# A list-scheduled decoder trunk: issue order by due times, other PSUM banks for one output projection, a token-tile-wise entry

## The chip, the cores and the metric

The kernel runs on one core of a Trainium2 chip. The metric is the device time of one execution in microseconds (us). Three executions of the kernel before took 1010.73, 1011.19 and 1012.37 us; their median, 1011.19 us, is the time that the change is compared with.

## The reference

The kernel computes a trunk of two layers on 256 tokens of 1024 channels, in float32. Each layer is an FFN, a token mixer and a second FFN; every one of these six parts reads a normalised copy of the residual stream h and adds a normalised result to it:

```python
def rms_norm(x, g):
    y = xf * lax.rsqrt(jnp.mean(xf * xf, axis=-1, keepdims=True) + NORM_EPS)
    return y * g
...
def swiglu(x, w_in, w_out):
    a, b = jnp.split(x @ w_in, 2, axis=-1)      # 1024 -> 2 * 2816
    return (jax.nn.silu(a) * b) @ w_out         # 2816 -> 1024
...
for l in range(DEPTH):                          # 2
    f = swiglu(rms_norm(h, g[0]), ffn1_w_in[l], ffn1_w_out[l])
    h = h + FFN_RES * rms_norm(f, g[1])
    hn = rms_norm(h, g[2])
    m = even_mixer(hn, ...) if l % 2 == 0 else odd_mixer(hn, ...)
    h = h + rms_norm(m, g[3])
    f = swiglu(rms_norm(h, g[4]), ffn2_w_in[l], ffn2_w_out[l])
    h = h + FFN_RES * rms_norm(f, g[5])
```

The even mixer is stick-breaking attention (8 heads) beside a causal depthwise convolution of width 31. The odd mixer is gated linear attention (4 heads, chunks of 64), whose output is normalised by head, multiplied by silu(r) and projected by w_out.

## The kernel before, in words

**Tiles.** The 256 tokens are two token tiles, A (t = 0) and B (t = 1), of 128 rows. Channels lie in eight blocks of 128. A float32 product is made of three fp32r matmuls (`mm3`, L334 to L336): high part by high part, low by high, high by low. So each weight tile of 128 x 1024 that arrives by DMA (raw, L318) is cast on ScalarE (ACT) to its high part (hi, L310), and VectorE (DVE) subtracts that from the tile to get the low part (lo, L311). Names in the trace follow: raw_fi, hi_fi and lo_fi are FFN input weights, fo its output weights, he and ho the even mixer's, gq, gv and gout the odd mixer's. Activations are split in the same way into uTh and uTl.

**Phases.** There are six: ffn0, even mixer, ffn1, ffn2, odd mixer, ffn3. In an FFN the first four of 22 column blocks are computed token-major: the matmuls fill a bank pt, the gate makes ut = silu(a) * b from it (ACT L582 or L587, DVE L584 or L588), TensorE (PE) transposes ut into a bank ptr (L595), and ACT and DVE split that into uTh and uTl. The other 18 blocks are computed channel-major into two banks pw_j0 and pw_j1 (L536 with the high weights, 512 columns; L538 with the low ones, 256 columns), gated through uab and uw, and split. The output projection o_f (L334 to L336) fills four banks, one for each token tile and half of the channels.

**Between the phases.** The post-norm of a token tile squares the four banks' halves on ACT (psq, L344), multiplies each half by the gain on DVE (py, L361), adds the two sums and eps (pst, L349), raises the sum to the power -1/2 on GpSimd (POOL, L340, a 128x1 tensor_tensor), and updates h (L367). The pre-norm then has the same chain (xsq, xst, the power, xn L467) and PE transposes xn into xT (xtr_p, L479).

**The entry.** ffn0 doesn't wait for statistics: class Entry multiplies the first four blocks by g * x^T, unnormalised (`split`: xgh L395 on ACT, xgl L397 on DVE, in blocks of 256 columns; matmuls pt<-hi_fi,xgh and so on), and the gate applies the row's rstd later. x itself (h) is loaded on the same DMA queue (`load_x`, L300), squared, and its rstd is laid out along rows by a matmul with the identity (rstd_rows, L425 and L427). `scaled` then multiplies x^T by gain and rstd (L432), casts (L442) and subtracts (L443); the channel-major blocks pw_40 and later read this xT.

**The odd mixer's end.** For each chunk and head the output bank go is squared (og L1064), its statistic gst gets eps (L1067) and the power (L340), sm = go * gst * rg (L1069), and sm is transposed (gt L1076) and split for the output projection o_go. Beside that DVE copies masked scores out of PSUM (COPY_PREDICATED, L1041).

**Memory rings.** PSUM has eight banks: four in the ring "out", two in the ring "in" (b0, b1; the projections' banks), two in the ring "tr" (b2, b3; transposes); channel-major blocks (ring "pw") take b0 to b3 in turn. Raw weights have four buffers, hi and lo parts nine.

**What sets the order.** The program isn't issued as it is written. Every step is recorded as an Op with an engine, a modelled cost in ns, the tiles it reads and writes, and a number i in program order. `Plan.schedule` then runs a list scheduler: the engine that can start earliest takes, among its ready steps (within a patience of some ns), the one with the lowest prio:

```python
o = min((o for o in ops if max(free[e], o.ready) <= t0 + o.patience), key=lambda o: o.prio)
```

prio is the number i, apart from a few steps that `urgent` sets ahead. The resulting order is fixed in the instruction streams: each engine and each queue works strictly in that order, and an instruction that waits holds all behind it on its engine. The costs and latencies of the model only choose the order.

## Time and profile before

| | |
|---|---|
| runs | 1010.73, 1011.19, 1012.37 us |
| the profiled execution | 1011.41 us |
| its span (first to last instruction on the core) | 1009.7 us |
| granted TensorE clock over the span, mean | 0.998 |
| PE busy | 992.0 us (98%) |
| DVE busy | 679.7 us (67%) |
| ACT busy | 568.0 us (56%) |
| POOL busy | 57.0 us (6%) |
| DMA | 180.46 MB, mean 179 GB/s |

The profile comes from one execution, which took 1011.41 us by the device's clock; 1.7 us of that lie outside the span. Busy times are sums of instruction durations; matmuls are pipelined, so the drawn end of one lies behind the start of the next. The chain that ended last follows the work back from the last instruction, at each step to what released it.

### The profile page before, as it was taken

Reading aid. Unit: us, or ns where it says so; the run is one execution under the profiler, and the core shown is the slowest. Engines: PE = TensorE matmul, PEld = TensorE weight load, DVE = VectorE, ACT = ScalarE, POOL = GpSimd, SP = SyncE. Lnnn points to the kernel's source line nnn. Section 1 sums busy time; section 2 is a strip of 40 time slices with the busy share of each in tenths; the row PEclk is TensorE's granted clock in tenths of the full one; section 3 lists DMA queues with packets and bytes.
Section 4 is the critical chain, followed back from the end, with each engine's and each line's share of the span. In section 5 each row is a group of like instructions: output and inputs, shape, how many; then the busy total and the mean of one; then the engine's idle time right before and its main releaser. Section 6 shows DMA issues by size and latency. Waiting matters only on the chain.

```text
span 1009.7 us, 13983 instructions
## 1 busy us (share of the span) xinstructions
PE 992.0 (98%) x5216; PEld 843.0 (83%) x5216; DVE 679.7 (67%) x1103; ACT 568.0 (56%) x979; POOL 57.0 (6%) x109
## 2 busy tenths in 40 slices
PE   7999999999999999999999999999999999999997
PEld 5888888888777888888888888888899887888885
DVE  5875668669868766667666566774588686656662
ACT  7764556575556655557455555664474375555551
POOL 2630000100001000000000000000001110000000
PEclk9999999999999999999999999999999999999999
DMA  9775557552035756566446465672551156555531
GB/s 326 236 249 191 191 203 258 184 184 68 22 126 167 255 170 221 166 211 228 169 161 216 167 218 161 228 267 69 191 205 64 42 188 230 187 188 191 198 112 42
DMA packets 50342, 180.46 MB, mean 179 GB/s; under 512 B 5713, under 2 KB 5969, under 8 KB 50274
## 3 DMA queue, kind: packets, MB, share of 16 engines
q1 hardware_dynamic: 50274, 179.57, 53.4%
q8 instruction: 41, 0.67, 0.3%
q14 instruction: 27, 0.22, 0.1%
HBM read 178.50 MB, written 1.05 MB: 178 GB/s over the span
## 4 chain that ended last, share of the span: by engine, by line
PE 90%; DVE 4%; DMA 2%; ACT 1%; issue 1%; POOL 1%; SPq 0%; DVEq 0%; POOLq 0%; ACTq 0%
PE pw L536 25%; PE pw L538 13%; PE o_f L334 8%; PE o_f L335 8%; PE o_f L336 8%; DMA raw_fi<-ffn_in 2%; PE pt L334 2%; PE pt L335 2%; PE pt L336 2%; PE gv L334 1%; PE gv L336 1%; PE gv L335 1%; PE cv L836 1%; PE xtr_p L479 1%; PE hq L334 1%
## 5 line engine op out<-in xcount | busy, mean ns | idle before, releaser
L536 PE MATMUL pw<-xT_p,hi_fi 128*128 128x512 f32 x1152 | 287.9, 392 | 2.3 <-DVE ut L588 1.3
L536 PEld LDWEIGHTS pw<-xT_p,hi_fi 128*128 128x128 f32 x1152 | 210.5, 188 | 43.8 <-DVE uTl L311 1.8
L311 DVE TENSOR_TENSOR lo_fi<-raw_fi,hi_fi 128x1024 fp32r<-128x1024 f32 (+1 forms) x177 | 212.8, 1217 | 47.8 <-ACT hi_fi L310 34.3
L310 ACT CAST hi_fi<-raw_fi 128x1024 fp32r<-128x1024 f32 (+1 forms) x177 | 181.4, 1046 | 40.1 <-DMA raw_fi<-ffn_in 19.4
L538 PEld LDWEIGHTS pw<-xT_p,lo_fi 128*128 128x128 f32 x1152 | 157.1, 190 | 11.3
L538 PE MATMUL pw<-xT_p,lo_fi 128*128 128x256 f32 x1152 | 160.6, 282 | 0.0
L662 DVE TENSOR_TENSOR uab<-pw,uab 128x256 f32<-128x256 f32 x144 | 60.8, 422 | 111.9 <-ACT uab L661 111.9
L661 ACT COPY uab<-pw 128x256 f32<-128x256 f32 x144 | 53.5, 372 | 130.7 <-PE pw L538 130.7
L334 PE MATMUL o_f<-hi_fo,uTh 128*128 128x512 f32 x224 | 88.2, 394 | 0.0
L335 PE MATMUL o_f<-lo_fo,uTh 128*128 128x512 f32 x224 | 87.8, 392 | 0.0
L336 PE MATMUL o_f<-hi_fo,uTl 128*128 128x512 f32 x224 | 87.2, 389 | 0.0
L311 DVE TENSOR_TENSOR lo_fo<-raw_fo,hi_fo 128x1024 fp32r<-128x1024 f32 x56 | 68.4, 1222 | 13.7 <-ACT uw L663 8.9
L310 ACT CAST hi_fo<-raw_fo 128x1024 fp32r<-128x1024 f32 x56 | 58.9, 1052 | 18.6 <-PE pw L536 11.9
L340 POOL TENSOR_TENSOR pst_p<-pst_p,mhalf 128x1 f32<-128x1 f32 x12 | 8.2, 685 | 783.5 <-DVE pst_p L349 768.8
L560 ACT CAST uTh<-uw 128x256 fp32r<-128x256 f32 x72 | 29.3, 407 | 38.8 <-DVE uw L664 38.6
L334 PE MATMUL o_f<-h_fo,uTh 128*128 128x512 f32 x128 | 50.8, 397 | 0.0
L336 PE MATMUL o_f<-h_fo,uTl 128*128 128x512 f32 x128 | 50.5, 395 | 0.0
L335 PE MATMUL o_f<-l_fo,uTh 128*128 128x512 f32 x128 | 50.5, 395 | 0.0
L336 PEld LDWEIGHTS o_f<-hi_fo,uTl 128*128 128x128 f32 x224 | 42.1, 188 | 9.2
L334 PEld LDWEIGHTS o_f<-hi_fo,uTh 128*128 128x128 f32 x224 | 42.3, 189 | 7.3
L335 PEld LDWEIGHTS o_f<-lo_fo,uTh 128*128 128x128 f32 x224 | 42.3, 189 | 6.7
L311 DVE TENSOR_TENSOR l_fo<-raw_fo,h_fo 128x1024 fp32r<-128x1024 f32 x32 | 39.1, 1223 | 10.0 <-ACT h_fo L310 9.7
(249 smaller groups left out, 1654.5 us busy)
## 6 DMA issues: line engine op xcount, KB each, us to landing
raw_fi<-ffn_in SPq DMA_DIRECT2D x176, 512.0 KB, 4.5
raw_fo<-ffn_out SPq DMA_DIRECT2D x88, 512.0 KB, 4.4
raw_gv<-gla_in SPq DMA_DIRECT2D x16, 512.0 KB, 4.6
...
```

Of the source, the lines that this page charges most:

```text
L310: act(n, lambda: nc.scalar.copy(hi(), src()), r, [w[0]], psum=psum)
L311: dve(n, lambda: nc.vector.tensor_sub(lo(), src(), hi().bitcast(F32)), list(r) + [w[0]], [w[1]])
L334: nc.tensor.matmul(ps, lhsT=lhs[0], rhs=rhs[0], start=start, stop=False)
L335: nc.tensor.matmul(ps, lhsT=lhs[0], rhs=rhs[1], start=False, stop=False)
L336: nc.tensor.matmul(ps, lhsT=lhs[1], rhs=rhs[0], start=False, stop=stop)
L479: nc.tensor.transpose(ps[:, k * P:(k + 1) * P], y[:, c * P:(c + 1) * P], ident[:, :])
L536: nc.tensor.matmul(pss[i][:, :], lhsT=wk, rhs=xT[:, k, :, :], start=k == 0, stop=False)
L538: nc.tensor.matmul(pss[i][:, S:], lhsT=wk, rhs=xT[:, k, 0, :], start=False, stop=k == KT - 1)
L560: act(n, lambda: nc.scalar.copy(h_[:, s], src()), r, [(h_, 0), (h_, 1)], psum=psum)
L661: act(S, lambda v=v, ps=ps: nc.scalar.copy(v(), ps[:, S:]), [ps], [(g, i)], psum=True)
L662: dve(S, lambda v=v, ps=ps: nc.vector.tensor_add(v(), ps[:, :S], v()), [ps, (g, i)], [(g, i)])
L836: nc.tensor.matmul(pv[:, :S], lhsT=d[:, o:o + P], rhs=pads(c)[:, i:i + S], start=i == 0, stop=i == CONV_PE - 1)
```

## The change

It has three parts.

1. **Order by due times.** After a first run in program order, `set_due` takes the PE order it gave, lays the PE steps end to end by their costs, and goes backward through all steps: a step is due when the earliest of its users is due, less the latency to that user and its own cost. prio of all steps but PE's becomes this due time, ties go by i, and the scheduler runs again; this is done twice (`PASSES`). PE keeps program order as its priority. Modelled constants change too: the latency from engine to engine from 80 to 150 ns, the one behind a DMA from 900 to 600, the DMA rate from 360 to 285 bytes per ns, the cost of the power from 470 to 690.
2. **Banks.** The output projection of the odd mixer takes tile A's two banks from the ring "in" in place of "out".
3. **Entry.** `split` works in halves of 512: ACT scales x^T in place by the gain (2 x 256), then one cast (512), and DVE subtracts once (512). `scaled` works by token tile: tile A's rstd_rows matmul, four-block products, casts and subtracts don't wait for tile B's. The product no longer has the gain in it, since x^T has it already. load_x(0) and load_x(1) stand around the weights of the second pair of blocks in program order.

```diff
+PASSES = 2
...
-    LATENCY = 80
-    DMA_START, DMA_DONE = 1700, 900
+    LATENCY = 150
+    DMA_START, DMA_DONE = 1700, 600
...
-        return self.add("dma", nbytes / 360.0, fn, r, w)
+        return self.add("dma", nbytes / 285.0, fn, r, w)
...
+        order = self.run()
+        for _ in range(PASSES):
+            self.set_due(order)
+            order = self.run()
+        return order
+
+    def latency(self, o, u):
+        lat = self.LATENCY if u.eng != o.eng or o.eng in ("act", "dve") else 0.0
+        return lat + (self.DMA_DONE if o.eng == "dma" else 0) + (self.DMA_START if u.eng == "dma" else 0)
+
+    def set_due(self, order):
+
+
+        t, begin = 0.0, {}
+        for o in order:
+            if not isinstance(o, str) and o.eng == "pe":
+                begin[o] = t
+                t += o.cost
+        for o in reversed(self.ops):
+            due = min((u.due - (self.latency(o, u) if o in u.deps else -o.cost) for u in o.users), default=t) - o.cost
+            o.due = min(due, begin.get(o, t))
+        for o in self.ops:
+            if o.eng != "pe":
+                o.prio = max(o.due, 0.0)
...
-                o = min((o for o in ops if max(free[e], o.ready) <= t0 + o.patience), key=lambda o: o.prio)
+                o = min((o for o in ops if max(free[e], o.ready) <= t0 + o.patience), key=lambda o: (o.prio, o.i))
...
-        gps(470, lambda: nc.gpsimd.tensor_tensor(st[:, 3:4], st[:, 2:3], mhalf[:, :], op=ALU.pow),
+        gps(690, lambda: nc.gpsimd.tensor_tensor(st[:, 3:4], st[:, 2:3], mhalf[:, :], op=ALU.pow),
...
-            for k in range(4 * b, 4 * b + 4):
-                act(S, lambda k=k: nc.scalar.activation(self.cols(hi, k), self.cols(raw, k), AF.Copy, scale=self.g(k)),
-                    [raw, self.gk], [(hi, k)], ptrs=1)
-                dve(S, lambda k=k: nc.vector.scalar_tensor_tensor(
-                    self.cols(lo, k), self.cols(raw, k), self.g(k), self.cols(hi, k).bitcast(F32),
-                    op0=ALU.mult, op1=ALU.subtract), [raw, self.gk, (hi, k)], [(lo, k)], ptr=True)
+            for i in range(2):
+                ks = (4 * b + 2 * i, 4 * b + 2 * i + 1)
+                s = slice(i * H, (i + 1) * H)
+                for k in ks:
+                    act(S, lambda k=k: nc.scalar.activation(self.cols(raw, k), self.cols(raw, k), AF.Copy, scale=self.g(k)),
+                        [(raw, i), self.gk], [(raw, i)], ptrs=1)
+                keys = [[(q, k) for k in ks] for q in (hi, lo)]
+                act(H, lambda s=s: nc.scalar.copy(hi[:, s], raw[:, s]), [(raw, i)], keys[0])
+                dve(H, lambda s=s: nc.vector.tensor_sub(lo[:, s], raw[:, s], hi[:, s].bitcast(F32)),
+                    [(raw, i), *keys[0]], keys[1])
...
-            for k in range(KT):
-                raw = self.raw[k // 4]
-                dve(S, lambda k=k, raw=raw: nc.vector.scalar_tensor_tensor(
...
+                   [(small, "1"), (small, t)], [(ps, t)])
+                for b in range(2):
+                    raw = self.raw[b]
+                    v = lambda raw=raw, c=c: raw[:, :].rearrange("p (k n) -> p k n", k=4)[:, :, c]
+                    xs = [lambda b=b, q=q, c=c: xT[:, b * 4:(b + 1) * 4, q, c] for q in range(2)]
+                    keys = [(xT, (q, t, b)) for q in range(2)]
+                    dve(H, lambda v=v, c=c: nc.vector.tensor_mul(
+                        v(), v(), ps[:, c].unsqueeze(1).broadcast_to([P, 4, P])), [raw, (ps, t)], [(raw, ("n", t))])
+                    act(H, lambda v=v, xs=xs: nc.scalar.copy(xs[0](), v()), [(raw, ("n", t))], [keys[0]])
+                    dve(H, lambda v=v, xs=xs: nc.vector.tensor_sub(xs[1](), v(), xs[0]().bitcast(F32)),
+                        [(raw, ("n", t)), keys[0]], [keys[1]])
...
+                            load_x(0)
                             ahead.append(blocks(1, 0))
+                            load_x(1)
...
-        banks = out_banks("go")
+        banks = out_banks("go", ("in", "out"))
```

What the three parts do to the order is seen in the instruction streams. Line numbers of the changed kernel are higher by some twenty: its lo subtracts are L333, ut is L609, the channel-major matmuls L557 and L559, o_f L356 to L358, gst L1090, sm L1092.

VectorE in ffn3, around ut_11, the last token-major gate product (uTl_0 reads the transposes ptr_10; lo_fi_6_0 and lo_fi_6_1 are low parts of the weights of block 6). Before:

```order
L311 TENSOR_TENSOR uTl_3_8069<-ptr_01_8036,uTh_3_8057 128x128
L311 TENSOR_TENSOR lo_fi_5_1_8079<-raw_fi_5_1_8034,hi_fi_5_1_8067 128x1024
L311 TENSOR_TENSOR lo_fi_6_0_8091<-raw_fi_6_0_8055,hi_fi_6_0_8081 128x1024
L311 TENSOR_TENSOR lo_fi_6_1_8104<-raw_fi_6_1_8071,hi_fi_6_1_8093 128x1024
L311 TENSOR_TENSOR uTl_0_7996<-ptr_10_8095,uTh_0_7993 128x128
L588 TENSOR_TENSOR ut_11_8108<-ut_11_8108,pt_11_8041 128x256
L311 TENSOR_TENSOR lo_fo_2_0_8125<-raw_fo_2_0_8089,hi_fo_2_0_8114 128x1024
L311 TENSOR_TENSOR uTl_1_8000<-ptr_10_8095,uTh_1_7998 128x128
```

And now:

```order
L333 TENSOR_TENSOR uTl_3_8069<-ptr_01_8034,uTh_3_8063 128x128
L333 TENSOR_TENSOR lo_fi_5_1_8079<-raw_fi_5_1_8037,hi_fi_5_1_8067 128x1024
L333 TENSOR_TENSOR lo_fi_6_0_8094<-raw_fi_6_0_8065,hi_fi_6_0_8087 128x1024
L609 TENSOR_TENSOR ut_11_8096<-ut_11_8096,pt_11_8041 128x256
L333 TENSOR_TENSOR uTl_0_7996<-ptr_10_8089,uTh_0_7993 128x128
L333 TENSOR_TENSOR lo_fi_6_1_8115<-raw_fi_6_1_8077,hi_fi_6_1_8104 128x1024
L333 TENSOR_TENSOR uTl_1_8020<-ptr_10_8089,uTh_1_8006 128x128
L333 TENSOR_TENSOR lo_fo_2_0_8131<-raw_fo_2_0_8092,hi_fo_2_0_8122 128x1024
L333 TENSOR_TENSOR lo_fo_2_1_8155<-raw_fo_2_1_8113,hi_fo_2_1_8141 128x1024
```

ut_11 stands ahead of uTl_0 and of lo_fi_6_1, which it followed; the same swap is found in ffn1 and ffn2.

TensorE in ffn3, where the first output products of block 0 end and the channel-major block 5 begins (pw_50 and pw_51 are its two banks). Before:

```order
L334 MATMUL o_f_8188<-hi_fo_0_0_8020,uTh_0_7993 128x512
L335 MATMUL o_f_8188<-lo_fo_0_0_8022,uTh_0_7993 128x512
L336 MATMUL o_f_8188<-hi_fo_0_0_8020,uTl_0_7996 128x512
L536 MATMUL pw_50_8196<-xT_p_7847,hi_fi_5_0_8050 128x512 x4
L536 MATMUL pw_50_8196<-xT_p_7847,hi_fi_5_1_8067 128x512 x4
L538 MATMUL pw_50_8196<-xT_p_7847,lo_fi_5_0_8059 128x256 x4
L538 MATMUL pw_50_8196<-xT_p_7847,lo_fi_5_1_8079 128x256 x4
L536 MATMUL pw_51_8221<-xT_p_7847,hi_fi_5_0_8050 128x512 x4
```

And now:

```order
L357 MATMUL o_f_8186<-lo_fo_0_0_8022,uTh_0_7993 128x512
L358 MATMUL o_f_8186<-hi_fo_0_0_8018,uTl_0_7996 128x512
L557 MATMUL pw_51_8191<-xT_p_7838,hi_fi_5_0_8050 128x512 x4
L557 MATMUL pw_50_8201<-xT_p_7838,hi_fi_5_0_8050 128x512 x4
L557 MATMUL pw_50_8201<-xT_p_7838,hi_fi_5_1_8067 128x512 x4
L559 MATMUL pw_50_8201<-xT_p_7838,lo_fi_5_0_8061 128x256 x4
L559 MATMUL pw_50_8201<-xT_p_7838,lo_fi_5_1_8079 128x256 x4
L557 MATMUL pw_51_8191<-xT_p_7838,hi_fi_5_1_8067 128x512 x4
L559 MATMUL pw_51_8191<-xT_p_7838,lo_fi_5_0_8061 128x256 x4
L559 MATMUL pw_51_8191<-xT_p_7838,lo_fi_5_1_8079 128x256 x4
```

Four matmuls into pw_51 have come ahead of pw_50, and the rest of pw_51 stays behind it.

VectorE at the end of the odd mixer, from a statistic gst to the product sm that it scales (lo_gout is the low part of an output weight). Before:

```order
L1019 TENSOR_TENSOR ex_7229<-ex_7229,gqk_7067 128x128
L1021 TENSOR_TENSOR ex_7229<-ex_7229,gqk_7067 128x128
L1067 TENSOR_SCALAR gst_7252<-gst_7252 128x1
L311 TENSOR_TENSOR lo_gout_0_7271<-raw_gout_0_7029,hi_gout_0_7256 128x1024
L1069 SCALAR_TENSOR_TENSOR sm_6585<-go_7233,gst_7252,rg_6856 128x256
L1041 COPY_PREDICATED sm_6588<-mk,sp_7262 128x128 x2
```

And now:

```order
L1090 TENSOR_SCALAR gst_7270<-gst_7270 128x1
L1042 TENSOR_TENSOR ex_7248<-ex_7248,gqk_7059 128x128
L1044 TENSOR_TENSOR ex_7248<-ex_7248,gqk_7059 128x128
L1064 COPY_PREDICATED sm_6588<-mk,sp_7278 128x128 x2
L1092 SCALAR_TENSOR_TENSOR sm_6585<-go_7252,gst_7270,rg_6854 128x256
L1064 COPY_PREDICATED sm_6588<-mk,sp_7278 128x128 x2
```

The subtract lo_gout has left the stretch between gst and sm; two ex products and two predicated copies stand there.

Four further moves, in words. In the last post-norm of each token tile DVE has py, pst, py, h in place of py, py, pst, h. The rstd_rows matmul of tile A stands six PE matmuls earlier than the pair did, and that of tile B 28 rows behind it, among the matmuls of the second pair of blocks. On DVE tile A's two products of `scaled` stand ahead of tile B's sum xst, which is followed there by two subtracts of xT and the subtract lo_fi_11_1; on ACT the casts of tile A's xT stand between and behind tile B's two squares. On SyncE's DMA queue the loads of h for tile A stand one weight load earlier, and those for tile B one later.

## Rows read from the trace of the kernel before

**Rows 1.** The page: busy time by engine, and the chain that ended last

```profile
PE 992.0 (98%) x5216; PEld 843.0 (83%) x5216; DVE 679.7 (67%) x1103; ACT 568.0 (56%) x979; POOL 57.0 (6%) x109
...
PE 90%; DVE 4%; DMA 2%; ACT 1%; issue 1%; POOL 1%; SPq 0%; DVEq 0%; POOLq 0%; ACTq 0%
```

**Rows 2.** Waits of TensorE: engine, line, releaser, total us, times, longest

```profile
PE pt L334 <- ACT hi_fi L310: 7.2, 1, 7.2
PE pw L536 <- DVE ut L588: 1.3, 3, 0.6
PE pw L536 <- DVE uTl L311: 1.0, 2, 0.6
PE gt L1076 <- DVE sm L1069: 0.7, 3, 0.3
PE xtr_p L479 <- DVE xn_p L467: 0.4, 2, 0.3
```

**Rows 3.** Timeline of TensorE at 849 us: start, us, engine, line, operation, out<-in

```profile
848.97 0.39 PE L335 MATMUL o_f<-lo_fo,uTh 128*128 128x512 f32 x1
849.21 0.39 PE L336 MATMUL o_f<-hi_fo,uTl 128*128 128x512 f32 x1
849.97 0.73 PE L536 MATMUL pw<-xT_p,hi_fi 128*128 128x512 f32 x2 [0.37 <-DVE uTl L311]
```

**Rows 4.** Timeline of VectorE at 848 us, the subtract ahead of uTl

```profile
848.49 1.22 DVE L311 TENSOR_TENSOR lo_fi<-raw_fi,hi_fi 128x1024 fp32r<-128x1024 f32 x1
```

**Rows 5.** Timeline of all engines, 840 to 843 us, around a wait for ut

```profile
839.93 2.50 DVE L311 TENSOR_TENSOR lo_fi<-raw_fi,hi_fi 128x1024 fp32r<-128x1024 f32 x2 [1.43 <-ACT hi_fi L310]
...
841.22 0.39 ACT L587 ACTIVATE ut<-pt 128x256 f32<-128x256 f32 x1
...
842.34 0.28 DVE L311 TENSOR_TENSOR uTl<-ptr,uTh 128x128 fp32r<-128x128 f32 x1
842.54 0.41 DVE L588 TENSOR_TENSOR ut<-ut,pt 128x256 f32<-128x256 f32 x1
...
843.10 0.47 PE L536 MATMUL pw<-xT_p,hi_fi 128*128 128x512 f32 x1 [0.59 <-DVE ut L588]
```

**Rows 6.** Timelines of VectorE and POOL, 759 to 765 us, around two powers

```profile
759.56 1.23 DVE L311 TENSOR_TENSOR lo_gout<-raw_gout,hi_gout 128x1024 fp32r<-128x1024 f32 x1
...
763.83 0.90 DVE L1041 COPY_PREDICATED sm<-mk,sp 128x128 f32<-128x128 uint32 x4
...
759.80 1.39 POOL L340 TENSOR_TENSOR gst<-gst,mhalf 128x1 f32<-128x1 f32 x1 [65.99 <-DVE gst L1067]
764.06 0.55 POOL L340 TENSOR_TENSOR gst<-gst,mhalf 128x1 f32<-128x1 f32 x1 [2.87 <-DVE gst L1067]
```

**Rows 7.** Timeline of all engines behind the last matmul

```profile
1003.02 1.41 DVE L361 TENSOR_TENSOR py_p<-o_f,gain 128x512 f32<-128x512 f32 x2 [7.50 <-ACT psq_p L344]
...
1004.34 0.15 DVE L349 SCALAR_TENSOR_TENSOR pst_p<-pst_p 128x1 f32<-128x1 f32 x1
1004.67 0.55 POOL L340 TENSOR_TENSOR pst_p<-pst_p,mhalf 128x1 f32<-128x1 f32 x1 [10.60 <-DVE pst_p L349]
1005.25 1.42 DVE L367 SCALAR_TENSOR_TENSOR h<-py_p,pst_p,h 128x512 f32<-128x512 f32 x2 [0.75 <-POOL pst_p L340]
```

**Rows 8.** Entry: timelines, loads of h, and the window's busy times and DMA share

```profile
4.73 1.70 ACT L395 ACTIVATE xgh<-x_t,g_first 128x256 fp32r<-128x256 f32 x4 [2.65 <-DMA g_first<-g_first]
6.54 1.14 ACT L310 CAST hi_fi<-raw_fi 128x512 fp32r<-128x512 f32 x2
...
22.24 0.60 PE L427 MATMUL rstd_rows<-entry_small 128*128 128x128 f32 x4
...
10.61 1.87 SPq L300 DMA_DIRECT2D h<-x  x4
...
h<-x SPq DMA_DIRECT2D x4, 256.0 KB, 6.5
...
0.00:30.00 30.00, 22.79 (x92) 18.13 (x93) 18.92 (x31) 20.99 (x36) 10.64 (x33) 1.00 0.82 296
```

More of the change, by code (lines that the diff above doesn't have):

```diff
@@ L59 @@
 class Op:
-    __slots__ = ("i", "eng", "cost", "fn", "deps", "queue", "prio", "table", "patience", "users", "wait", "ready", "end")
+    __slots__ = ("i", "eng", "cost", "fn", "deps", "queue", "prio", "table", "patience", "users", "wait", "ready", "end", "due")
     def __init__(self, i, eng, cost, fn, prio, table, patience):
@@ L153, in schedule, with run @@
             op.queue -= op.deps
-            op.wait, op.ready = len(op.deps) + len(op.queue), 0.0
             for d in op.deps | op.queue:
                 d.users.append(op)
+        order = self.run()
[18 more added lines that the diff above has]
+                o.prio = max(o.due, 0.0)
+    def run(self):
+        for op in self.ops:
+            op.wait, op.ready = len(op.deps) + len(op.queue), 0.0
         cand = {e: [] for e in ("pe", "act", "dve", "gps", "dma")}
@@ L407, in statistics @@
         def statistics(self):
-            for t in range(NT):
-                load_x(t)
             for t in range(NT):
@@ L428, in scaled @@
                                                             start=True, stop=True),
-                   [(small, "1"), (small, t)], [ps])
-            for k in range(KT):
-                raw = self.raw[k // 4]
-                dve(S, lambda k=k, raw=raw: nc.vector.scalar_tensor_tensor(
-                    self.cols(raw, k), self.cols(raw, k), self.g(k), ps[:, :S], op0=ALU.mult, op1=ALU.mult),
-                    [raw, self.gk, ps], [raw], ptr=True)
-                if k % 4 == 3:
-                    b = k // 4
-                    def part(q, b=b):
-                        return xT[:, b * 4:(b + 1) * 4, q, :]
-                    v = lambda raw=raw: raw[:, :].rearrange("p (k n) -> p k n", k=4)
-                    keys = [[(xT, (q, t, b)) for t in range(NT)] for q in range(2)]
-                    act(D, lambda p=part, v=v: nc.scalar.copy(p(0), v()), [raw], keys[0])
-                    dve(D, lambda p=part, v=v: nc.vector.tensor_sub(p(1), v(), p(0).bitcast(F32)),
-                        [raw, *keys[0]], keys[1])
+                   [(small, "1"), (small, t)], [(ps, t)])
[9 more added lines that the diff above has]
+                        [(raw, ("n", t)), keys[0]], [keys[1]])
     def new_xT(name):
@@ L546, in out_proj, with out_banks @@
            [(aT[0], t), (aT[1], t), *w], [bk], loads=3)
-    def out_banks(name):
-        return [[bank("out", f"o_{name}{t}{n}") for n in range(2)] for t in range(NT)]
+    def out_banks(name, rings=("out", "out")):
+        return [[bank(rings[t], f"o_{name}{t}{n}") for n in range(2)] for t in range(NT)]
     def new_uT(name):
```

9 lines of the change are left out of this document (2 added, 7 removed).

## The prediction

> **What bounds the kernel now.** I read the busy times and the chain that ended last first. The reader is to see that TensorE (PE) is busy for 992.0 of the span's 1009.7 us and that 90% of the chain is its own work [rows 1]. The change leaves the number of PE matmul rows as it is, but for one split (below), so it can move only what PE doesn't spend on matmuls: 17.7 us. Second I read what PE waits for [rows 2]: 7.2 us at the start, before the first weights are cast, and ten listed waits of 1.3 + 1.0 + 0.7 + 0.4 = 3.4 us: for a gate product (ut, three), for the low part of a transposed product (uTl, two), for the normalised output of the gated mixer (sm, three), for the normed activations (xn, two). The rest, 17.7 - 7.2 - 3.4 = 7.1, is the tail behind the last matmul [rows 7] with crumbs.
>
> Third I read two successive matmuls, to learn what a wait really costs [rows 3]. A 512-column matmul is shown 0.39 long, yet the next one starts 0.23 to 0.24 later (848.97 to 849.21). So its drawn end lies 0.16 behind the point where PE could have gone on, and a listed wait costs its length plus 0.16: at 849.21 the next start comes 0.76 later, so 0.53 is lost, and 0.37 is listed. That is the price rule of every wait below.
>
> **Part 1, the order by due times.** *Waits for ut (three, 1.3 listed).* On VectorE (DVE) the product ut stands behind two 1024-wide subtracts (2.50 us for the pair) and the uTl that reads the other transposes [rows 5]: the silu it needs starts on ScalarE at 841.22 and takes 0.39, so it could run from about 841.6, but starts at 842.54, and PE's next block follows at 843.10. In the new order ut stands in front of one of the two subtracts and of uTl, in all three of the FFN phases with this wait. One subtract is 1.25, and the uTl 0.28, so ut comes up to 1.5 earlier where at most 0.6 + 0.16 is lost: all of it goes. Gain 1.3 + 3 x 0.16 = **1.8**; lower bound 0.6, if the next wait of the same queue (uTl, now behind ut, 0.41 later) takes two thirds of it.
>
> *Waits for uTl (two, 1.0 listed).* PE's block pw_50 takes the PSUM bank that the last transposes occupy until uTl has read them; the uTl stands behind a 1.22 us subtract that began at 848.49 [rows 4], so PE resumes 0.76 after 849.21 [rows 3]. In the new order four matmuls of pw_51, in another bank, come ahead of pw_50: at 0.23 each, 0.9 of cover for 0.53 (and for at most 0.6 + 0.16). Gain 1.0 + 2 x 0.16 = **1.3**; lower bound 0.5, if one of the two comes back elsewhere.
>
> *Waits for sm (three, 0.7 listed).* sm needs a reciprocal root which GpSimd (POOL) takes as a power. Beside a subtract with both inputs in SBUF (759.56, 1.23 long) that power takes 1.39, until 0.40 behind the subtract's end; beside copies from PSUM (763.83) it takes 0.55 [rows 6]. The new order puts no subtract between the statistic gst and sm at the place that the change shows, so 0.84 is saved where about 0.4 is lost. Gain 0.7 + 3 x 0.16 = **1.2**, lower bound 0.4 (one of three). The Trainium skill ("SBUF — State Buffer", section "Who interferes with whom") gives the reason: a DVE instruction with two SBUF inputs shares the read path with a GpSimd instruction that reads SBUF, and whoever issues first shuts the other out; with at most one SBUF input there is no contention. By that rule, the trace agrees: 1.39 against 0.55.
>
> *Waits for xn (two, 0.4 listed).* The statistic, power and xn chain is the same kind. At the second token tile a lo subtract still stands beside the power in the new order, so I count 0.4 + 2 x 0.16 less one 0.16: **0.6**, bounds 0 and 0.9 (0.84 is what one unlocked power gives back).
>
> *The tail.* Nothing follows the last post-norm. Today DVE does two products py of 0.7 each from 1003.02, then the sum pst (1004.34, 0.15), then POOL the power (1004.67, 0.55), then h at 1005.25 [rows 7]. In the new order pst precedes the second py: it starts at 1003.02 + 0.70 = 1003.72, 0.62 earlier, and the power then runs beside the second py (0.7), which reads PSUM, like the copies of [rows 6]. h starts at about 1004.63. Gain **0.6**. Lower bound: if the py did lock the power out, it would end 0.40 after a py that ends at 1004.5, gaining 0.3.
>
> **Part 2, the gated mixer's banks.** Tile A's output projection takes banks of the input ring, so PE can start it before the last go banks are free. It moves six matmuls and more forward among the small fp32 ones; no row shows what it saves beyond the sm waits. Bounds: a gain as large again as these (0.7), a loss as large as the longest wait (0.6). I take 0, since the matmuls are the same and only the three sm waits are listed in that stage [rows 2].
>
> **Part 3, the entry.** *First matmul.* The weights' cast that releases PE (hi_fi, 6.54) follows four scale ACTIVATEs (from 4.73, 1.70 together) with 0.11 to spare [rows 8]. Now the four scales are followed by a 512-wide cast ahead of hi_fi, 0.57 by the halves of hi_fi (1.14 for two). So PE starts 0.57 - 0.11 = 0.46 later; DVE, one 512-wide subtract instead of four products, makes up a little. Cost **+0.4**, bounds 0 and +0.6. Later halves have whole weight blocks between them and PE, so they cost nothing; were that cover gone, one cast and one subtract are about 1.2.
>
> *The row scales.* Today both tiles' rstd_rows run at 22.24, after both tiles' squares [rows 8]. Now tile A's rows stand six matmuls earlier in PE's queue (1.4 at 0.23 each; with the 0.4 of the later start that is 21.2), tile B's 27 matmuls behind these, at about 27.5. Tile B's power stands beside two subtracts of xT and a lo subtract, all with two SBUF inputs, so by [rows 6] it loses 0.84, or more if the second subtract shuts it out too; between its squares and its row scale ScalarE's queue holds casts of xT that wait for tile A's rows. Bounds 0 (5.3 us later than today is enough) and +1.0 (the 0.84 and an issue gap, with nothing to spare). I take **+0.3**, nearer to the hidden end, because 5.3 is much against 0.84. [...]
>
> *SP's queue.* The loads of h for tile A move ahead of one weight load, tile B behind the next; they issue at 10.61 now and take 6.5 to land [rows 8]. Weight loads that slip by two 256 KB loads still have a ring of four in front.
>
> **Sum.** -1.8 - 1.3 - 1.2 - 0.6 - 0.6 + 0.4 + 0.3 = -4.8. The span goes from 1009.7 to 1004.9; the profiled execution from 1011.41 to 1006.6. The median of the runs, 1011.19, lies 0.2 below it, so I predict **1006.4**.
>
> **The rivals.** *(A) The forecast*: own range 1004.9 (no start cost, xn at 0.9, some crumbs) to 1007.8 (entry at its upper bounds, 0.9; half the xn and tail gain).
>
> *(B) Waits change place.* Engines issue in fixed order, so a step that goes forward pushes another back: with the lower bounds for ut, uTl and sm (0.6 + 0.5 + 0.4), 0.3 for xn, 0.2 for the tail and +0.7 for the entry the sum is -1.3; the middle between that and the forecast is -3.0. Taken at about -2.6: **1008.6**. For it: five of the terms have a lo subtract next in line. Against it: the ten waits average 0.34 us, a third of a subtract.
>
> *(C) The due times miss.* They come from costs and a modelled PE order; if these are off by as much as a wait (0.3 to 0.6), new waits as many as the old ones arise and nothing moves: about **1011**, within 2.0 either way. Against it: the pairs of rows in the order do swap as the waits ask.
>
> *(D) Slower: the x loads.* PE's queue is fixed, and tile A's rows now stand ahead of the second half of the entry's weights. Its h loads share a queue that is 0.82 busy in the first 30 us [rows 8]. Today they issue from 10.61, land at about 17.1, and the rows of both tiles run 5.1 later. One weight load earlier, each released by a subtract of 1.23 [rows 6], is about 9.4; for one tile alone I take some 3 of those 5.1, so they must land by about 18.2 for PE's place at 21.2. At 6.5 us they land at 15.9. Each us beyond 18.2 costs one; 2.0 is lost net of the gains only beyond 18.2 + 4.8 + 2.0 = 25.0, that is, 15.6 us after issue: then **1013.4** or more. For it: the busy queue. Against it: that is 2.4 times today's landing time.
>
> **How the numbers follow.** Measurement can tell 0.2% (2.0 us) from no change, so faster is below 1009.2, slower above 1013.2. Chances: A 0.57, B 0.24, C 0.14, D 0.05. Faster is A, and most of B (0.20) = 0.77; same is the rest of B and most of C = 0.17; slower is D and a little of C = 0.06. The range that leaves out 2 in 10 holds A and B's bulk: 1003.8 (a part of A with some 1.1 us of waits that aren't listed) to 1009.8.
>
> **What would show it.** In the profile after: no PE wait for ut, and none for uTl over 0.2; sm's power at 0.55 instead of 1.39; h of the tail about 0.6 earlier behind the last matmul; PE's first matmul at 7.5 to 7.7 rather than 7.2. PE should idle about 13 us, not 17.7. The prediction is wrong if PE's busy time itself changes by over 1 us, if the listed waits reappear under other names with 3 us or more, or if a wait of over 1 us for rstd_rows stands between 20 and 30 us.

## The result, and the profile after

The changed kernel took 1004.35 us (median of five, 1004.02 to 1005.18) beside 1011.14 for the kernel before (median of five): a ratio of 0.993, 95% interval 0.9919 to 0.9941. That is 6.8 us less, inside the range forecast (1003.8 to 1009.8), faster as in the likeliest case, but 2.0 below its 1006.4 and 0.5 below that case's own range. The profiled execution has a span of 1002.6 against 1009.7. First the page of the changed kernel, busy times and chain, beside [rows 1]:

```profile
span 1002.6 us, 13984 instructions
...
PE 988.2 (99%) x5216; PEld 843.7 (84%) x5216; DVE 678.0 (68%) x1097; ACT 568.1 (57%) x985; POOL 55.6 (6%) x109
...
PE 98%; DMA 1%; DVE 1%; ACT 0%; POOL 0%; issue 0%; SPq 0%; DVEq 0%; POOLq 0%; ACTq 0%
```

PE is the whole chain now (98%, it was 90%), and 14.4 us of the span lie outside its busy time in place of 17.7. That busy time fell by 3.8 us, though no matmul row has gone; the section on the prediction comes back to it. Its waits (engine, line, releaser, total us, times, longest) answer to [rows 2]:

```profile
PE pt L356 <- ACT hi_fi L332: 7.9, 1, 7.9
PE xtr_p L500 <- DVE xn_p L488: 0.4, 1, 0.4
```

The waits for ut, uTl and sm are gone; one for xn is left. The timeline behind the last matmul, beside [rows 7]:

```profile
996.60 0.69 DVE L383 TENSOR_TENSOR py_p<-o_f,gain 128x512 f32<-128x512 f32 x1 [8.13 <-ACT psq_p L366]
...
997.32 0.16 DVE L371 SCALAR_TENSOR_TENSOR pst_p<-pst_p 128x1 f32<-128x1 f32 x1
997.40 0.68 DVE L383 TENSOR_TENSOR py_p<-o_f,gain 128x512 f32<-128x512 f32 x1
997.62 0.55 POOL L362 TENSOR_TENSOR pst_p<-pst_p,mhalf 128x1 f32<-128x1 f32 x1 [10.60 <-DVE pst_p L371]
998.21 1.41 DVE L389 SCALAR_TENSOR_TENSOR h<-py_p,pst_p,h 128x512 f32<-128x512 f32 x2
```

pst (997.32) stands between the two products py now, and the power, 0.55, runs beside the second: h starts 998.21 - 996.07 = 2.14 after the start of the last matmul (it was 1005.25 - 1002.49 = 2.76). Last, ScalarE's and PE's timeline at the entry, beside [rows 8]:

```profile
6.28 0.60 ACT L424 CAST xgh<-x_t 128x512 fp32r<-128x512 f32 x1
...
7.22 1.14 ACT L332 CAST hi_fi<-raw_fi 128x512 fp32r<-128x512 f32 x2 [0.34 <-DMA raw_fi<-ffn_in]
...
7.89 0.80 PE L356 MATMUL pt<-hi_fi,xgh 128*128 128x512 f32 x1 [7.89 <-ACT hi_fi L332]
```

The cast hi_fi that releases PE did not wait for the new 512-wide cast ahead of it, which ended at 6.88, but for the landing of its weights (DMA raw_fi). In the odd mixer the powers that sm needs took 0.66, 0.66 and 0.55 (1.39, 1.39 and 1.59 before) at the three places where PE had waited for sm.

**Where the time went.** PE's first matmul starts at 7.89 (7.21 before), its last at 996.07 (1002.49), and the span ends 6.57 behind that (7.19). So the stretch between first and last matmul is 988.18 long, 7.10 less than 995.28. From the matmul records I added up what each step to the next start is longer than the median step of its shape. These excesses fall from 26.96 to 20.16 us, in these places:

| stretch, us | before | after | what stood there before |
|---|---|---|---|
| 0 to 40 | 3.08 | 3.09 | the first matmuls, up to 0.7 apart and mostly 0.43 |
| 40 to 60 | 1.00 | 0.06 | wait for uTl |
| 60 to 300 | 9.32 | 9.39 | |
| 300 to 360 | 2.00 | 1.18 | waits for xn, one for ut |
| 500 to 560 | 0.84 | 0.33 | wait for ut |
| 740 to 800 | 5.18 | 2.68 | waits for sm, switches between small matmuls and o_go |
| 800 to 860 | 2.43 | 0.34 | waits for xn, ut, uTl |

In the first row the granted clock of the profile reads 1.00 in both kernels, so these rows don't say why the first matmuls are slow. The other stretches keep theirs within 0.1; the last 0.3 is a median step of the 128-column matmuls that is 1 ns shorter.

### The profile page after: what moved, and what is told of

The parts are those of the page before. It is cut to its first block, busy times and chain, and to the rows that moved or that the text cites. A ratio compares the mean times of both kernels' runs of the same rounds, so it can differ in the third digit from the quotient of the medians.

```text
span 1002.6 us, 13984 instructions
## 1 busy us (share of the span) xinstructions
PE 988.2 (99%) x5216; PEld 843.7 (84%) x5216; DVE 678.0 (68%) x1097; ACT 568.1 (57%) x985; POOL 55.6 (6%) x109
## 4 chain that ended last, share of the span: by engine, by line
PE 98%; DMA 1%; DVE 1%; ACT 0%; POOL 0%; issue 0%; SPq 0%; DVEq 0%; POOLq 0%; ACTq 0%
PE pw L557 26%; PE pw L559 14%; PE o_f L356 8%; PE o_f L357 8%; PE o_f L358 8%; PE pt L356 3%; PE pt L357 3%; PE pt L358 3%; PE gv L357 1%; PE gv L358 1%; PE gv L356 1%; PE sp L1060 1%; PE cv L859 1%; PE hq L356 1%; PE xtr_p L500 1%; PE gq L356 1%
## 5 line engine op out<-in xcount | busy, mean ns | idle before, releaser
L557 PE MATMUL pw<-xT_p,hi_fi 128*128 128x512 f32 x1152 | 287.0, 392 | 0.0
L557 PEld LDWEIGHTS pw<-xT_p,hi_fi 128*128 128x128 f32 x1152 | 211.0, 189 | 40.0
L333 DVE TENSOR_TENSOR lo_fi<-raw_fi,hi_fi 128x1024 fp32r<-128x1024 f32 (+1 forms) x177 | 213.0, 1217 | 45.2 <-ACT hi_fi L332 31.9
L559 PEld LDWEIGHTS pw<-xT_p,lo_fi 128*128 128x128 f32 x1152 | 157.0, 191 | 11.0
L559 PE MATMUL pw<-xT_p,lo_fi 128*128 128x256 f32 x1152 | 160.4, 283 | 0.0
L356 PE MATMUL o_f<-hi_fo,uTh 128*128 128x512 f32 x224 | 88.3, 394 | 0.0
L358 PE MATMUL o_f<-hi_fo,uTl 128*128 128x512 f32 x224 | 87.3, 390 | 0.0
L333 DVE TENSOR_TENSOR lo_fo<-raw_fo,hi_fo 128x1024 fp32r<-128x1024 f32 x56 | 68.4, 1221 | 14.5 <-ACT uw L686 8.0
L356 PE MATMUL o_f<-h_fo,uTh 128*128 128x512 f32 x128 | 50.8, 397 | 0.0
L358 PE MATMUL o_f<-h_fo,uTl 128*128 128x512 f32 x128 | 50.6, 395 | 0.0
L358 PEld LDWEIGHTS o_f<-hi_fo,uTl 128*128 128x128 f32 x224 | 42.2, 188 | 9.2
L356 PEld LDWEIGHTS o_f<-hi_fo,uTh 128*128 128x128 f32 x224 | 42.3, 189 | 7.2
L333 DVE TENSOR_TENSOR l_fo<-raw_fo,h_fo 128x1024 fp32r<-128x1024 f32 x32 | 39.2, 1224 | 5.5 <-ACT h_fo L332 5.1
```

What stands on the lines that cost most here:

```text
L333: dve(n, lambda: nc.vector.tensor_sub(lo(), src(), hi().bitcast(F32)), list(r) + [w[0]], [w[1]])
L356: nc.tensor.matmul(ps, lhsT=lhs[0], rhs=rhs[0], start=start, stop=False)
L358: nc.tensor.matmul(ps, lhsT=lhs[1], rhs=rhs[0], start=False, stop=stop)
L557: nc.tensor.matmul(pss[i][:, :], lhsT=wk, rhs=xT[:, k, :, :], start=k == 0, stop=False)
L559: nc.tensor.matmul(pss[i][:, S:], lhsT=wk, rhs=xT[:, k, 0, :], start=False, stop=k == KT - 1)
```

## Experiments

All in one table; "PE" is the time from the start of the first matmul to the start of the last in the profiled execution, which leaves out the start and the tail, and is of one execution each. Every ratio was taken against the kernel before, run beside that version; its medians lie between 1010.6 and 1011.1. So two versions differ for certain only where their intervals don't overlap.

| kernel | median us (range) | ratio to before, interval | PE |
|---|---|---|---|
| before | 1010.6 to 1011.1 | 1 | 995.3 |
| changed | 1004.35 (1004.02 to 1005.18) | 0.993, 0.9919 to 0.9941 | 988.2 |
| e1 constants alone | 1011.38 (1010.86 to 1012.31) | 1.0009, 1.0000 to 1.0017 | 994.8 |
| e2 due times alone | 1010.41 (1009.08 to 1012.47) | 0.9997, 0.9988 to 1.0005 | 994.7 |
| e3 banks alone | 1009.89 (1009.26 to 1011.59) | 0.9994, 0.9985 to 1.0003 | 993.0 |
| e12 entry alone | 1012.39 (1011.63 to 1013.91) | 1.0018, 1.0009 to 1.0027 | 995.0 |
| e5 without due times | 1010.45 (1009.61 to 1010.89) | 0.9992, 0.9983 to 1.0001 | 992.7 |
| e6 without new constants | 1011.48 (1010.22 to 1012.31) | 1.0003, 0.9994 to 1.0012 | 995.5 |
| e7 without new entry | 1008.56 (1007.87 to 1009.03) | 0.9974, 0.9965 to 0.9984 | 991.8 |
| e8 without new banks | 1006.92 (1005.58 to 1007.26) | 0.9958, 0.9946 to 0.9971 | 990.1 |
| e9 old DMA constants | 1006.16 (1005.53 to 1007.08) | 0.9957, 0.9944 to 0.9969 | 989.5 |
| e4 old split in the new entry | 1005.91 (1005.33 to 1007.18) | 0.9954, 0.9941 to 0.9966 | 990.5 |
| e10 guard for the power | 1005.04 (1004.06 to 1006.70) | 0.9948, 0.9934 to 0.9961 | 988.3 |
| e11 first loads in halves | 1003.63 (1002.92 to 1003.79) | 0.9929, 0.9916 to 0.9941 | 988.4 |

The first question was which part of the order carries it: the constants (theory C) or the due times (theory D).

**e1, the constants alone** (the kernel before, plus):

```diff
-    LATENCY = 80
-    DMA_START, DMA_DONE = 1700, 900
+    LATENCY = 150
+    DMA_START, DMA_DONE = 1700, 600
-        return self.add("dma", nbytes / 360.0, fn, r, w)
+        return self.add("dma", nbytes / 285.0, fn, r, w)
-        gps(470, lambda: nc.gpsimd.tensor_tensor(st[:, 3:4], st[:, 2:3], mhalf[:, :], op=ALU.pow),
+        gps(690, lambda: nc.gpsimd.tensor_tensor(st[:, 3:4], st[:, 2:3], mhalf[:, :], op=ALU.pow),
```

> The kernel before with the modelled constants of the change alone (latency 150, DMA 600 and 285, power 690), scheduled once in program order, old entry, old banks. Theory C (the constants carry the order's gain): with them pw_51 already goes ahead of pw_50, no lo_gout stands between gst and sm, and ut_11 stands before lo_fi_6_1; so the waits for ut, uTl and sm go (1.8, 1.5 and 1.2 us) with some 1 us of crumbs in the odd mixer, and the tail stays: about 1005.8 us. Theory D (the due times carry it): 1010 to 1011 us.

Measured 1011.38, no gain. PE's waits in e1:

```profile
PE xtr_p L501 <- DVE xn_p L489: 1.2, 1, 1.2
PE go L1081 <- DVE uTl_og L333: 1.2, 1, 1.2
PE pc L824 <- DVE e L819: 1.1, 2, 0.5
PE pt L357 <- DVE lo_fi L333: 0.8, 2, 0.5
PE pt L358 <- DVE xT_p L333: 0.2, 1, 0.2
```

Theory C is right about the waits it names and wrong about the time. Not one wait for ut, uTl of the FFN or sm is left, as the order said. But 4.5 us of others stand there: 1.2 for xn, 1.2 of go for uTl_og, 1.1 for e, 0.8 for low parts of weights.

**e2, the due times alone** (the kernel before, plus `set_due` and two passes).

> The kernel before with the two due-time passes alone, old constants, old entry, old banks. Theory C: only the tail (0.7) and part of the ut waits go (ut_11 passes uTl_0 but stays behind lo_fi_6_1), lo_gout stays between gst and sm, pw_50 stays ahead of pw_51: about 1009.5 us, with listed waits for sm and uTl as before. Theory D: 1005 to 1006 us.

Measured 1010.41, no gain that can be told. PE's waits in e2:

```profile
PE xtr_p L501 <- DVE xn_p L489: 1.5, 5, 0.4
PE gt L1098 <- DVE sm L1091: 0.5, 2, 0.3
PE pw L558 <- DVE ut L610: 0.4, 1, 0.4
```

One ut wait and two sm waits are still there, and xn has five waits in place of two. That with the old costs a step counts as due later than it is needed would explain it; this was not tried by itself. The uTl waits shrank to 0.15 at 848.97, against theory C. Both theories fell: neither carries it alone.

**e3, the banks alone** (the kernel before, plus the two lines on `out_banks`).

> The kernel before with tile A's output-projection banks of the gated mixer from the input ring, nothing else. 15 matmuls of the projection come earlier. If the banks pay by themselves, PE idles less between 785 and 802 us: up to 1 us, about 1010.2 us. If, as predicted, they only move work, 1011 us within 0.4.

Measured 1009.89; the interval holds 1. The excess in 780 to 800 us is 2.12 against 2.99, the 0.9 that "pay by themselves" asked for, but the time doesn't clear the noise. The trace shows something else. Its orders outside the odd mixer's end are those of the kernel before, row by row, and still the waits for ut near 342 and 528 and those for uTl are gone. The same order waits in one execution and not in another: 1.4 of the 2.3 us by which PE's time is shorter here are not the banks'. PE's start differs as well:

```profile
7.43 2.31 ACT L310 CAST hi_fi<-raw_fi 128x512 fp32r<-128x512 f32 x3 [1.15 <-DMA raw_fi<-ffn_in]
```

The cast for the first matmul waited 1.15 for its weights, where it waited for nothing that the profile lists in [rows 8]; PE starts at 8.10 here, 7.21 there, with the same entry code.

**e4, the old split in the new entry** (the changed kernel; the parts are made as before, and raw is scaled behind them):

```diff
-                act(H, lambda s=s: nc.scalar.copy(hi[:, s], raw[:, s]), [(raw, i)], keys[0])
-                dve(H, lambda s=s: nc.vector.tensor_sub(lo[:, s], raw[:, s], hi[:, s].bitcast(F32)),
...
+                act(S, lambda k=k: nc.scalar.activation(self.cols(hi, k), self.cols(raw, k), AF.Copy, scale=self.g(k)),
+                    [(raw, i), self.gk], [(hi, k)], ptrs=1)
...
+        def gained(self, b):
+            raw = self.raw[b]
+            for k in range(4 * b, 4 * b + 4):
+                act(S, lambda k=k: nc.scalar.activation(self.cols(raw, k), self.cols(raw, k), AF.Copy, scale=self.g(k)),
+                    [raw, self.gk], [raw], ptrs=1)
```

> The changed kernel with the entry's high part made again by one scaling ACTIVATE for each block and the low part by one DVE instruction for each block, as before; the scaling in place that the later token-tile steps need comes as eight more ACTIVATEs of 256 columns behind them. Theory Q (the cast in ScalarE's queue delays the first matmul): it starts at 7.2 us as before instead of 7.9, and the time is about 1003.7 us. Theory L (the first weights landed later in that execution): the first matmul starts when its weights land, at 7.5 to 7.9, and the time stays at 1004.3 us. If the eight added ACTIVATEs (3.3 us) are not hidden, the row scales come late and it is slower than 1004.4 us.

Measured 1005.91. PE starts at 8.37, released by weights that landed late: theory L, in an execution in which the cast couldn't have mattered. (Where the weights land early it does; see e10 in the section on the prediction.) The eight added ACTIVATEs were not hidden: PE waits 1.3 for xT at 34.7 (an excess of 1.44, most of the 1.6 us lost).

The next four undo one part each. The theories were now I (the parts pay only together) and E (banks and entry carry it).

**e5, without due times** (`PASSES = 0`).

> The changed kernel without the two due-time passes (program order as priority, all else kept). Theory I (constants and due times pay only together: the constants' order gains some 4.5 us in the FFN and sm waits and gives it back in new waits for xn, uTl_og and lo_fi, as in e1, which the due times prevent): 1009 to 1011 us, with new waits for xn of about 1.2 and for uTl_og of about 1.2, and the tail 0.7 longer. Theory E (banks and entry carry what e1 and e2 don't show): about 1005 us.

Measured 1010.45. PE's waits in e5:

```profile
PE xtr_p L500 <- DVE xn_p L488: 1.5, 2, 1.2
PE pc L825 <- DVE e L820: 1.1, 2, 0.5
PE pt L357 <- DVE lo_fi L333: 0.8, 2, 0.7
```

The new waits of e1 stand here again (1.5, 1.1, 0.8), but the one of go for uTl_og doesn't: the banks have taken it (it is back in e8, without them). So of what the constants' order gives back, the due times prevent some 3 us of listed waits; PE's time differs by 4.5 from the changed kernel's.

**e6, without the new constants** (80, 900, 360 and 470 again).

> The changed kernel with the constants of before (latency 80, DMA 900 and 360, power 470), due passes, banks and entry kept. Theory I: lo_gout returns between gst and sm, pw_50 stays ahead of pw_51, several xn waits of 0.3: 1009 to 1010.5 us. Theory E: about 1005 us.

Measured 1011.48, even above the forecast: xn 1.5 in five waits, ut 0.6, uTl 0.5, sm 0.5.

**e7, without the new entry** (old `split` and `scaled`, both loads of h in `statistics`).

> The changed kernel with the entry of before (split by blocks of 256, both token tiles scaled together, loads of h where they were). Theory I: the entry moves nothing behind 40 us, so 1004 to 1005.2 us. Theory E: the entry is what gains, 1007 us or more.

Measured 1008.56, where theory E put it; theory I's figure missed by some 4. That the entry gains by itself, as theory E has it, is another question: e12 below answers it. PE, DVE and then the windows (us, PE busy, PEld, DVE, ACT, POOL, PEclk, DMA share, GB/s) of e7:

```profile
35.93 4.62 PE L558 MATMUL pw<-xT_p,hi_fi 128*128 128x512 f32 x12 [1.77 <-DVE xT_p L465]
```

```profile
29.99 3.22 DVE L454 SCALAR_TENSOR_TENSOR x_t<-x_t,g_first,rstd_rows 128x256 f32<-128x256 f32 x8 [5.54 <-PE rstd_rows L449]
33.13 0.48 DVE L606 SCALAR_TENSOR_TENSOR ut<-pt,xst_p,ut 128x256 f32<-128x256 f32 x1
33.53 1.21 DVE L333 TENSOR_TENSOR lo_fi<-raw_fi,hi_fi 128x1024 fp32r<-128x1024 f32 x1
34.66 2.35 DVE L465 TENSOR_TENSOR xT_p<-x_t,xT_p 128x1024 fp32r<-128x1024 f32 x2
```

```profile
34.00:36.00 2.00, 0.23 (x3) 0.07 (x1) 2.00 (x3) 2.00 (x4) 2.00 (x1) 1.00 0.16 31
36.00:38.00 2.00, 2.00 (x6) 1.56 (x7) 2.00 (x2) 1.80 (x4) 2.00 (x1) 0.60 0.59 231
38.00:40.00 2.00, 2.00 (x7) 1.58 (x6) 2.00 (x6) 0.53 (x2) 1.64 (x2) 0.55 0.39 119
40.00:42.00 2.00, 2.00 (x14) 1.81 (x13) 1.99 (x5) 0.46 (x2) 0.00 (x0) 1.00 0.89 283
```

DVE's products wait for the rows of both tiles until 29.99; from there the eight of them (3.22), the casts and the first subtract of xT last until 35.8, and pw_40 waits 1.77 for that. Then the granted clock, a mean over each window, reads 0.60 and 0.55 of full speed for 36 to 40 us: from 36.59 seven matmuls go 0.43 apart in place of 0.23, the spacing at the 1.2 GHz level, 7 x 0.20 = 1.4 more. The excess in 20 to 40 us is 4.24 against 0.35.

**e8, without the new banks** (`out_banks("go")`).

> The changed kernel with tile A's banks of the gated output projection from the output ring again. Theory I with the 0.9 us that e3's trace shows less in 780 to 800 us: about 1005.2 us, with a wait of PE or its equal in matmul steps between 780 and 800 us; all else as in the changed kernel. Theory E: 1007 us or more.

Measured 1006.92, again nearer to theory E's figure than to theory I's. PE and DVE of e8 at 782 us:

```profile
783.29 0.70 PE L1082 MATMUL go<-gv,sm 128*128 128x256 f32 x2 [1.15 <-DVE uTl_og L333]
```

```profile
780.51 0.28 DVE L333 TENSOR_TENSOR uTl_og<-gt,uTh_og 128x128 fp32r<-128x128 f32 x1
781.81 1.23 DVE L333 TENSOR_TENSOR lo_fi<-raw_fi,hi_fi 128x1024 fp32r<-128x1024 f32 x1 [1.01 <-ACT hi_fi L332]
782.95 0.28 DVE L333 TENSOR_TENSOR uTl_og<-gt,uTh_og 128x128 fp32r<-128x128 f32 x1
```

And the same place in the changed kernel:

```profile
782.61 0.39 PE L358 MATMUL o_go<-hi_gout,uTl_og 128*128 128x512 f32 x1
782.83 0.62 PE L1082 MATMUL go<-gv,sm 128*128 128x256 f32 x2
```

```profile
781.28 1.23 DVE L333 TENSOR_TENSOR lo_fi<-raw_fi,hi_fi 128x1024 fp32r<-128x1024 f32 x1 [1.01 <-ACT hi_fi L332]
782.42 0.28 DVE L333 TENSOR_TENSOR uTl_og<-gt,uTh_og 128x128 fp32r<-128x128 f32 x1
```

DVE does the same in both: a subtract lo_fi, then uTl_og, which empties the bank that go takes. In e8 PE has nothing else and waits 1.15; in the changed kernel the six o_go matmuls that the banks let through fill 1.4 us there. The excess in 780 to 800 is 3.92 against 1.43, more than the 1.9 that PE loses in all.

**e12, the entry alone** (the kernel before, plus the new entry).

> The kernel before with the new entry alone (halves, token tile by token tile, loads of h around the second pair of blocks), old constants, no due times, old banks. Theory I (each part alone gains nothing, because the wait that it prevents isn't there without the others): no wait of PE for xT at 30 to 36 us in this order, as in the kernel before, so 1010.3 to 1011.5 us with the listed waits for ut, uTl and sm as before. Theory E (the entry pays by itself what its absence costs in e7, about 4 us): 1007 us.

Measured 1012.39, slower by 0.18%. There is no gain, as theory I said (its figure was 0.9 too low): PE is busy without a gap from 20 to 40 us, as before the change, so there is nothing to gain, and ut and uTl have waits up to 0.8 and 1.0. PE's time is no longer than before (995.0); what shows is the start, 0.8 later at 7.97. In this order two of the new casts stand ahead of hi_fi, which follows them without a listed wait (so it does in e5):

```profile
6.28 1.12 ACT L424 CAST xgh<-x_t 128x512 fp32r<-128x512 f32 x2
7.31 1.13 ACT L332 CAST hi_fi<-raw_fi 128x512 fp32r<-128x512 f32 x2
```

What the other half of the loss of 1.6 us is stays open.

**e9, the old DMA constants alone** (900 and 360).

> The changed kernel with the two DMA constants of before alone (900 behind a DMA, 360 bytes per ns); latency 150, power 690, due times, banks and entry kept. Theory R (the DMA rate is what makes the scheduler treat weight parts as late, and so lets ut and uTl pass them): pw_50 is ahead of pw_51 again and lo_fi_6_1 ahead of ut, so waits for ut and uTl of 0.4 to 0.8 each come back: 1006 to 1009 us. Theory P (power and latency do it): 1004 to 1005 us.

Measured 1006.16. The rows came back as theory R said (pw_50 ahead of pw_51, lo_fi_6_1 ahead of ut), the waits did not: 0.2 us is listed in all, for something else. The 1.3 us of PE lie in small excesses (0.98 against 0.31 in 300 to 320, 0.48 against 0.16 in 520 to 540). Which constant does what stays undecided: latency and power were not tried by themselves.

**e10, a guard for the power** (the changed kernel; in `run`, where `two` marks the subtracts of weights and `eps` the sums pst and xst):

```diff
+        at = lambda e, o: max(free[e], o.ready, hold if o.two else 0.0)
...
+            if o.eps:
+                hold = o.end + 700.0
```

> The changed kernel with one rule more in the scheduler: behind the sum that a post-norm or pre-norm hands to POOL (pst, xst), no weight subtract starts on VectorE for 0.7 us, so that none stands beside the power. If a subtract with two SBUF inputs is what makes the power 1.4 us, the powers at about 310 and 320 us fall to 0.55, the xn wait at 321.5 (0.53 in matmul steps) goes, and the time is about 1003.8 us. If the subtracts that wait now come late elsewhere, 1004.4 or more with new waits for lo_fi.

Measured 1005.04, no gain; the interval overlaps that of the changed kernel. The powers at the same place, in the changed kernel and in e10, and what DVE does beside the last:

```profile
310.11 1.47 POOL L362 TENSOR_TENSOR xst_p<-xst_p,mhalf 128x1 f32<-128x1 f32 x1 [2.73 <-DVE xst_p L371]
...
319.98 1.40 POOL L362 TENSOR_TENSOR xst_p<-xst_p,mhalf 128x1 f32<-128x1 f32 x1 [3.18 <-DVE xst_p L371]
```

```profile
309.02 0.55 POOL L368 TENSOR_TENSOR xst_p<-xst_p,mhalf 128x1 f32<-128x1 f32 x1 [2.73 <-DVE xst_p L377]
...
319.71 0.55 POOL L368 TENSOR_TENSOR xst_p<-xst_p,mhalf 128x1 f32<-128x1 f32 x1 [4.31 <-DVE xst_p L377]
```

```profile
319.42 0.15 DVE L377 SCALAR_TENSOR_TENSOR xst_p<-xst_p 128x1 f32<-128x1 f32 x1
319.62 0.42 DVE L615 TENSOR_TENSOR ut<-ut,pt 128x256 f32<-128x256 f32 x1
319.96 1.22 DVE L339 TENSOR_TENSOR lo_fi<-raw_fi,hi_fi 128x1024 fp32r<-128x1024 f32 x1
```

The cause is shown: with no subtract ahead of it the power takes 0.55 in place of 1.40 to 1.47, and the wait for xn goes. The gain isn't: the excess in 300 to 340 falls from 1.08 to 0.90, in 800 to 840 it rises from 0.26 to 1.14, most of it in steps into matmuls that read lo_fi.

**e11, the first loads in halves** (the changed kernel; weight tile and x^T tile 0 in two DMAs each, the second half of x^T behind the second weight tile):

```diff
-            dma(P * D * 4, lambda: nc.sync.dma_start(self.raw[b][:, :], x_t[b]), [], [self.raw[b]])
+            for i in range(2):
+                s = slice(i * H, (i + 1) * H)
+                o = dma(P * H * 4, lambda s=s: nc.sync.dma_start(self.raw[b][:, s], x_t[b][:, s]), [], [(self.raw[b], i)])
+                o.late = 0.5 if b == 0 and i == 1 else 0.0
...
+            if first and not i:
+                for n in range(2):
+                    s = slice(n * H, (n + 1) * H)
+                    dma(P * H * 4, lambda i=i, raw=raw, s=s: nc.sync.dma_start(raw[:, s], src[i][:, s]), [], [(raw, n)])
```

> The changed kernel with the first x^T tile and the first weight tile loaded in two halves each, the second half of x^T behind the second weight tile, so that the first matmul needs 0.5 MB rather than 1 MB. If the landing of the first tiles sets the start (it lay at 7.2 to 8.9 us, released by DMA in all but one of the traces), PE starts at 6 to 6.5 us and the time is about 1003 us. If ScalarE's queue sets it, it stays at 6.9 or more, and if the later weights land no earlier PE waits for them: 1004.3 us.

Measured 1003.63; its slowest run, 1003.79, is below the fastest of the changed kernel, 1004.02. ScalarE and PE at its start:

```profile
3.72 0.91 ACT L430 ACTIVATE x_t<-x_t,g_first 128x256 f32<-128x256 f32 x2 [1.63 <-DMA g_first<-g_first]
5.16 0.62 ACT L333 CAST hi_fi<-raw_fi 128x512 fp32r<-128x512 f32 x1 [0.54 <-DMA raw_fi<-ffn_in]
5.69 0.61 ACT L433 CAST xgh<-x_t 128x512 fp32r<-128x512 f32 x1
```

```profile
6.35 0.80 PE L362 MATMUL pt<-hi_fi,xgh 128*128 128x512 f32 x1 [6.35 <-ACT xgh L433]
```

The first weights land by 5.16, and PE starts at 6.35; the first matmuls' steps of 0.43 end 1.4 earlier too, and the span, 1001.3, is 1.3 shorter. It beats the kernel before. That it beats the changed kernel is likely but not shown: the two were run in different rounds, and their ratios, 0.9929 and 0.993, have almost the same interval.

## Why the prediction was right, and where it was off

| term | forecast | measured (steps over the median) |
|---|---|---|
| three ut waits | -1.8 | 0.62 + 0.43 + 0.75 gone: -1.8 |
| two uTl waits | -1.3 | 0.79 + 0.53 gone: -1.3 |
| three sm waits | -1.2 | 0.38 + 0.46 + 0.33 gone: -1.2 |
| rest of the odd mixer | 0 (-0.7 to +0.6) | 2.50 - 1.17: -1.3 |
| xn | -0.6 | 1.40 to 0.70: -0.7 |
| tail | -0.6 | 7.19 to 6.57: -0.6 |
| first matmul | +0.4 | 7.21 to 7.89: +0.7, but not by the cause named |
| row scales of the entry | +0.3 | 0 |
| other steps | none | -0.8: 0.5 in small excesses, 0.3 in the median step of 128 columns |
| sum | -4.8 | -7.0 |

The price rule (listed wait plus 0.16) and the four terms read from waits held to 0.1 each, and so did the tail: these mechanisms were right, and of the waits only one for xn is left, as was forecast. That they fit to 0.1 is partly luck, for each side is one execution, and e3's, with the order of the kernel before in the FFNs, lacks both waits for uTl and two of the three for ut. What such an execution loses to them on the average isn't known. Three sizes failed.

- *"It moves six matmuls and more forward among the small fp32 ones; no row shows what it saves beyond the sm waits. ... I take 0, since the matmuls are the same ..."* The stretch gave 1.3 beyond the sm waits, outside the bounds of -0.7 and +0.6. The bounds took listed waits only; the excesses of 0.1 to 0.2 at each switch between o_go and the small matmuls, which no wait row lists, were left out. e3 and e8 show what the banks do: 0.9 alone, 2.5 in the new order, where they cover a wait that the order itself would make.
- *"So PE starts 0.57 - 0.11 = 0.46 later."* The step lacks a condition, that the weights have landed. In both profiles the chain that ended last begins with their landing, 4.80 behind the issue at 1.71 before and 5.48 now. So the 0.7 between the two starts is a later landing; and before, hi_fi (6.54) stood right behind its weights (6.51) rather than behind ScalarE's queue. In e10, which has the changed kernel's entry, the weights were early, the chain begins with the gains (g_first), and hi_fi follows the new cast without a wait:

```profile
6.29 0.60 ACT L430 CAST xgh<-x_t 128x512 fp32r<-128x512 f32 x1
6.80 1.14 ACT L338 CAST hi_fi<-raw_fi 128x512 fp32r<-128x512 f32 x2
```

```profile
7.46 0.79 PE L362 MATMUL pt<-hi_fi,xgh 128*128 128x512 f32 x1 [7.46 <-ACT hi_fi L338]
```

PE starts at 7.46 there, 0.25 later than before. So the cast has a price where the weights are early, 0.25 in place of 0.46, and none where they are late. The starts of all traces, 7.2 to 8.4 with the old split and 7.5 to 8.9 with the new one (6.35 with half loads aside), spread too widely to show it.
- *Row scales, +0.3.* Tile B's power took 0.93 (26.08 to 27.01) and nobody waited: the 5.3 us of slack were the right argument. Two subtracts of 512 columns stood beside it from 25.91 to 27.20, and it ended before the second did: that it loses "more if the second subtract shuts it out too" did not come true.

One of the prediction's own signs of being wrong did appear: PE's busy time changed by 3.8 us where over 1 was to refute it, and PE idles 14.4 us, not about 13. The sign was ill chosen. By the price rule every wait that goes takes 0.16 of drawn busy time with it, 1.4 for nine waits, and steps that are slow without a listed wait count as busy, 1.3 in the odd mixer. The other signs held, but for the first matmul's place, and sm's power stayed at 0.66 in two of three places, each time with an ex product (both inputs in SBUF) that had begun before it.

The xn term was right for its reason: the wait left at 321.54 (0.53) stands behind a power of 1.40 beside a subtract, and e10 takes it away.

What the forecast didn't see at all is how the parts hang together. It added up prices as if each part earned its own; the sum came out within its range, since it was read from the order of all parts together. But alone the constants, the due times and the banks earn nothing that can be told and the entry loses 1.6, and without constants or due times nearly everything is lost (e5, e6). Added up, taking one part away costs 6.1 + 7.1 + 4.2 + 2.6 = 20 us, three times the gain of all together. Constants and due times together, without banks and entry, were not run. Rival B, "waits change place", is what each part does by itself: e1 removes the waits it aims at and makes as many others. Rival C, due times that miss, is what e2 and e6 look like: with the old constants nothing is gained. Of rival D there is no sign: the changed kernel lists no wait of PE for rstd_rows.
